# Softmax over the row dot products of two batches: VectorE sums all 32 rows of a step

## The chip, the core and the metric

The kernel runs on one core of a Trainium2 chip. The core has several engines that run their own instruction streams and meet at semaphores: VectorE (DVE in the profile) and ScalarE (ACT) do the arithmetic here, SyncE (SP) orders the transfers between the chip's memory (HBM) and the on-chip memory, and 16 DMA engines carry them out. TensorE is not used. On-chip memory has 128 partitions; a tile of 128 x 512 has 512 elements in each.

The metric is the device time of one execution in microseconds, as a median over runs.

## The reference

```python
B, N, D = 8, 4096, 512          # x and y: B x N x D, float32
gram = np.matmul(x, y.transpose(0, 2, 1))
diag = np.diagonal(gram, axis1=1, axis2=2)
diag = diag - diag.max(axis=-1, keepdims=True)
exp = np.exp(diag)
return (exp / exp.sum(axis=-1, keepdims=True)).astype(np.float32)
```

Only the diagonal of the product is kept, so what is computed is, for each of 8 x 4096 rows, the dot product of a row of x with the same row of y (512 elements), and then a softmax over the 4096 values of each batch. Both inputs, 134 MB together, have to be read once; the output has 0.13 MB.

## The kernel before

Four batches are worked on at a time. A batch's 4096 rows are spread over a quadrant of 32 partitions, 128 rows to a partition (C = 128), so that the four batches fill 128 partitions. Two such groups of batches make the whole. A step t takes R = 32 rows of each partition; there are S = 8 steps, 0 to 3 for the first group and 4 to 7 for the second. A step loads 32 x 512 elements per partition of x (8.4 MB over all partitions) and as much of y.

Buffers: x has two buffers (xs, used in turn: t % 2), y has one (ys). A small buffer, side, holds the last K = 6 rows of y of a step. The tile diag holds the dot products, 128 columns per group; res holds the results.

Steps 0 to 5 are the loop at L133. In each of them

- SyncE orders the load of x (L71) into the buffer of this step, and then the load of y (L74). Both are on one queue, in the order of the program. The order of x waits until the sums of step t - 2, which read the same buffer, are done; the order of y waits until the first multiply of step t - 1 and the copy to side have read ys.
- ScalarE copies the last 6 rows of y to side (L136), as soon as y has landed.
- VectorE multiplies the first 26 rows of x by y, in place (L78, 13,312 elements per partition), and then the last 6 rows by side (L78, 3,072 elements). So ys is free after the first of the two.
- The products are summed along each row. VectorE sums rows 0 to 29 in one instruction (sums, L81, a reduce of 15,360 elements per partition to 30 values). ScalarE sums rows 30 and 31 (sums_act, L86; W = 2), each with one activation that copies the row onto itself and accumulates, and an instruction that reads the accumulator out to diag.

Behind the sums of step 3 VectorE takes the maximum of the first group (L106, L100) and ScalarE the exponentials (L113); step 4 begins on VectorE with the normalization (L100, L119, L120).

Steps 6 and 7 stand outside the loop. In step 6 the rows of y that are kept aside go to the part of the other x buffer that step 7 fills last (spare, L150), and ScalarE sums 30 rows, VectorE two. The first piece of x of step 7 (15 rows) is ordered, as in the loop, when the sums of step 5 are done. Step 7 loads x and y in pieces and takes the dot products row by row on VectorE (L89), so that little is left to do when the last piece lands. Then the second group's softmax and the stores follow.

The instructions of each engine run in the order in which the program writes them; nothing reorders them. An order of a transfer that has to wait holds up what SyncE orders behind it.

Of the kernel before, what the change touches and what calls it, by code (L numbers as in the profile page):

```python
# [11 lines left out]
def kernel(  # L12
# [17 lines left out]
    R = 32  # L30
    H = R // 2
    K = 6
    W = 2
# [30 lines left out]
    def rows(t, r0, n):  # L64
        return xs[t % 2][:, r0 : r0 + n, :]

    def dots_of(t, r0, n):
        return diag[t * R // C][:, columns(t, r0, n)]

    def load_x(t, r0, n):  # L70
        nc.sync.dma_start(out=rows(t, r0, n), in_=xv[t * R // C, :, columns(t, r0, n), :])  # L71

    def load_y(t, r0, n):
        nc.sync.dma_start(out=ys[:, r0 : r0 + n, :], in_=yv[t * R // C, :, columns(t, r0, n), :])  # L74

    def products(t, r0, n, yt):
        xt = rows(t, r0, n)
        nc.vector.tensor_tensor(out=xt, in0=xt, in1=yt, op=Alu.mult)  # L78

    def sums(t, r0, n):  # L80
        nc.vector.tensor_reduce(out=dots_of(t, r0, n), in_=rows(t, r0, n), axis=X, op=Alu.add)  # L81

    def sums_act(t, r0, n):
        for r in range(r0, r0 + n):
            row = xs[t % 2][:, r, :]
            nc.scalar.activation(out=row, in_=row, func=Act.Copy, accum_out=dots_of(t, r, 1))  # L86
# [21 lines left out]
    def exps(i, d):  # L108
        mxp = small.tile([P, 1], f32, name=f"mxp{i}")
        largest(mxp, d)  # L110
        nmx = over_quadrant(f"nmx{i}", mxp, Alu.max, negate=True)
        sump = small.tile([P, 1], f32, name=f"sump{i}")
        nc.scalar.activation(out=res[i], in_=diag[i][:, :C], func=Act.Exp, bias=nmx, scale=1.0, accum_out=sump)  # L113
        return sump

    def normalize(i, sump):
        total = over_quadrant(f"sum{i}", sump, Alu.add)
        rc = small.tile([P, 1], f32, name=f"rc{i}")
        nc.vector.reciprocal(out=rc, in_=total)  # L119
        nc.vector.tensor_single_scalar(out=res[i], in_=res[i], scalar=rc, op=Alu.mult)  # L120
# [12 lines left out]
    for t in range(S - 2):  # L133
        load_x(t, 0, R)
        load_y(t, 0, R)
        nc.scalar.activation(out=side, in_=ys[:, R - K :, :], func=Act.Copy)  # L136
        if t == C // R:
            normalize(0, sump)
        products(t, 0, R - K, ys[:, : R - K, :])
        products(t, R - K, K, side)  # L140
        sums(t, 0, R - W)
        sums_act(t, R - W, W)
        if t == C // R - 1:
            sump = exps(0, diag[0])

    t = S - 2
# [78 lines left out]
```

## Time and profile before

| | |
|---|---|
| Median of 3 runs | 319.71 us |
| Runs, lowest to highest | 319.66 to 319.84 us |
| Span of the profiled execution | 318.4 us |
| HBM read over the span | 134.22 MB, 422 GB/s |

The page gives no other time of the profiled execution than its span, from the first to the last instruction; the runs' times hold what lies ahead of it and behind it as well, 1.3 us more at the median.

The page begins with the busy time of each engine and the span in 40 slices: each digit is the busy share of a slice in tenths, 9 is 90% or more. For the DMA line that is the mean over the 16 DMA engines. "q1" is the queue on which all loads run. The chain of waits follows the work that ended last back from the last instruction: each piece is work, or a wait for a transfer. A transfer's piece in it runs from its order to its landing, and that includes the time in which it stands in the queue behind others.

In the views that group instructions a row has the line, the engine, the operation, output and input tile, shapes and count; then busy time and mean ns of one, and the idle time just before them. In the view in order of time a row starts with start and duration in us; idle time before the instruction stands in brackets at the end with what ended it.

### The profile page before, as it was taken

What the parts mean: (1) busy time and instruction counts of PE and PEld (TensorE: products, weight loads), DVE (VectorE), ACT (ScalarE), POOL (GpSimd) and SP (SyncE); (2) the same over time, 40 slices, a digit from 0 to 9 for tenths busy, and PEclk for the clock granted to TensorE, in tenths of its full rate; (3) what the DMA queues carried; (4) which work ended last, traced back from release to release, by engine and by line L of the source; (5) the groups of instructions that cost most, each with busy time, mean ns of one, the idle gap of its engine ahead of it and who ended that gap; (6) DMA issues with size and microseconds to landing.
All of it is one profiled execution on the core that took longest, in us unless ns stands there. A gap on an engine that the chain in (4) does not pass through costs nothing.

```text
span 318.4 us, 320 instructions
## 1 busy us (share of the span) xinstructions
DVE 241.7 (76%) x101; ACT 49.8 (16%) x97; POOL 0.2 (0%) x4
## 2 busy tenths in 40 slices
DVE  0000079994899939999399994999939998499995
ACT  1000030100301003010020102101030100496700
POOL 0000000000000000000000000000000000000000
DMA  9999999999999999999999999999999999999993
GB/s 397 395 395 510 412 395 453 469 395 395 486 436 395 453 469 395 395 486 436 395 395 519 403 395 461 461 395 395 527 395 395 486 436 395 425 415 432 434 410 140
DMA packets 3970, 134.37 MB, mean 422 GB/s; under 512 B 512, under 2 KB 896, under 8 KB 1536
## 3 DMA queue, kind: packets, MB, share of 16 engines
q1 hardware_dynamic: 3824, 134.29, 97.9%
q10 hardware_dynamic: 144, 0.07, 0.1%
q14 instruction: 2, 0.02, 0.0%
HBM read 134.22 MB, written 0.13 MB: 422 GB/s over the span
## 4 chain that ended last, share of the span: by engine, by line
DMA 70%; DVE 28%; issue 0%; SPq 0%; ACT 0%; DVEq 0%
DMA ys<-in_y_dram 59%; DVE xs L78 28%; DMA xs<-in_x_dram 11%; DVE xs L89 0%; SPq L74 0%; SPq L71 0%; DVE res L120 0%; DVE nmx L100 0%; DVE sum L100 0%; ACT res L113 0%; DVE mxp L106 0%; DVE rc L119 0%; DVEq L78 0%; DVEq L89 0%; SPq L131 0%
## 5 line engine op out<-in xcount | busy, mean ns | idle before, releaser
L78 DVE TENSOR_TENSOR xs<-xs,ys 128x13312 f32<-128x13312 f32 (+2 forms) x8 | 96.7, 12091 | 70.3 <-DMA ys<-in_y_dram 70.3
L81 DVE TENSOR_REDUCE diag<-xs 128x30 f32<-128x15360 f32 (+1 forms) x7 | 98.1, 14020 | 0.2
L86 ACT ACTIVATE xs<-xs 128x512 f32<-128x512 f32 x42 | 25.9, 617 | 90.4 <-DVE xs L78 90.4
L136 ACT ACTIVATE side<-ys 128x3072 f32<-128x3072 f32 x6 | 16.6, 2763 | 124.5 <-DMA ys<-in_y_dram 124.5
L89 DVE SCALAR_TENSOR_TENSOR xs<-xs,ys 128x512 f32<-128x512 f32 (+2 forms) x33 | 20.0, 669 | 0.8 <-DMA ys<-in_y_dram 0.7
L78 DVE TENSOR_TENSOR xs<-xs,side 128x3072 f32<-128x3072 f32 x6 | 20.1, 3350 | 0.0
L86 ACT ACTIVATION_READ_ACCUMULATOR xs<-xs 128x1 f32 x42 | 7.8, 187 | 0.0
L150 ACT ACTIVATE xs<-ys 128x4608 f32<-128x4608 f32 x1 | 4.0, 4043 | 19.9 <-DMA ys<-in_y_dram 19.9
L113 ACT ACTIVATE res<-diag,nmx 128x128 f32<-128x128 f32 x2 | 0.8, 401 | 29.8 <-DVE nmx L100 29.8
L78 DVE TENSOR_TENSOR xs<-xs,xs 128x4608 f32<-128x4608 f32 x1 | 5.0, 4951 | 0.0
L89 DVE DVE_READ_ACCUMULATOR xs<-xs,ys 128x1 f32 x33 | 2.7, 81 | 0.0
L124 ACT ACT_TABLE_LOAD x1 | 1.3, 1283 | 0.7 <-PEq L209 0.7
L100 DVE TRANSPOSE_TENSOR_REDUCE sum<-sump 128x1 f32<-128x32 f32 x2 | 0.4, 212 | 1.2 <-ACT res L113 1.2
L128 DVE MEMSET ys<- 128x1 f32 x1 | 0.1, 59 | 1.4 <-PEq L209 1.4
L120 DVE TENSOR_SCALAR res<-res,rc 128x128 f32<-128x128 f32 x2 | 0.6, 286 | 0.1
L106 DVE TENSOR_REDUCE mxp<-diag 128x1 f32<-128x128 f32 (+1 forms) x2 | 0.5, 228 | 0.1
L100 DVE TRANSPOSE_TENSOR_REDUCE nmx<-mxp 128x1 f32<-128x32 f32 x2 | 0.4, 212 | 0.1
L106 DVE TENSOR_REDUCE diag<-diag 128x1 f32<-128x64 f32 (+1 forms) x2 | 0.4, 202 | 0.0
L119 DVE RECIPROCAL rc<-sum 128x1 f32<-128x1 f32 x2 | 0.3, 164 | 0.1
L113 ACT ACTIVATION_READ_ACCUMULATOR res<-diag,nmx 128x1 f32 x2 | 0.4, 186 | 0.0
L189 ACT ACTIVATE met<-diag 128x96 f32<-128x96 f32 x1 | 0.3, 282 | 0.0
L209 POOL MEMSET const-bfloat16-1.0<- 128x1 bf16 x1 | 0.1, 101 | 0.0
(3 smaller groups left out, 0.3 us busy)
## 6 DMA issues: line engine op xcount, KB each, us to landing
ys<-in_y_dram SPq DMA_DIRECT2D x1, 4352.0 KB, 14.8
xs<-in_x_dram SPq DMA_DIRECT2D x1, 3840.0 KB, 14.1
ys<-in_y_dram SPq DMA_DIRECT2D x1, 2304.0 KB, 12.2
xs<-in_x_dram SPq DMA_DIRECT2D x1, 2048.0 KB, 19.3
xs<-in_x_dram SPq DMA_DIRECT2D x1, 1536.0 KB, 15.5
ys<-in_y_dram SPq DMA_DIRECT2D x1, 768.0 KB, 16.9
ys<-in_y_dram SPq DMA_DIRECT2D x3, 256.0 KB, 18.2
xs<-in_x_dram SPq DMA_DIRECT2D x1, 608.0 KB, 18.0
```

Of the source, the lines that this page charges most:

```text
L78: nc.vector.tensor_tensor(out=xt, in0=xt, in1=yt, op=Alu.mult)
L81: nc.vector.tensor_reduce(out=dots_of(t, r0, n), in_=rows(t, r0, n), axis=X, op=Alu.add)
L86: nc.scalar.activation(out=row, in_=row, func=Act.Copy, accum_out=dots_of(t, r, 1))
L89: nc.vector.scalar_tensor_tensor(out=xt, in0=xt, scalar=1.0, in1=yt, op0=Alu.mult, op1=Alu.mult, accum_out=out)
L100: nc.vector.tensor_reduce(out=got, in_=column.to_broadcast([P, G]), axis=X, op=op, negate=negate, apply_transpose=True)
L106: nc.vector.tensor_reduce(out=out, in_=d, axis=X, op=Alu.max)
L113: nc.scalar.activation(out=res[i], in_=diag[i][:, :C], func=Act.Exp, bias=nmx, scale=1.0, accum_out=sump)
L119: nc.vector.reciprocal(out=rc, in_=total)
L120: nc.vector.tensor_single_scalar(out=res[i], in_=res[i], scalar=rc, op=Alu.mult)
L124: nc.scalar.preload_act_table(Act.Exp)
L136: nc.scalar.activation(out=side, in_=ys[:, R - K :, :], func=Act.Copy)
L150: nc.scalar.activation(out=spare, in_=ys[:, F - L : F, :], func=Act.Copy)
```

## The change

In steps 0 to 5 VectorE's sum covers all 32 rows of the step instead of the first 30, and ScalarE's two row sums are taken out. The loads, the multiplies, the copy to side, steps 6 and 7 and the softmax stay as they are.

```diff
         products(t, 0, R - K, ys[:, : R - K, :])
         products(t, R - K, K, side)
-        sums(t, 0, R - W)
-        sums_act(t, R - W, W)
+        sums(t, 0, R)
         if t == C // R - 1:
             sump = exps(0, diag[0])
```

The reduce of a step has 16,384 elements per partition instead of 15,360 and writes 32 values. In six steps 12 activations and 12 accumulator reads go.

## The prediction

> **What bounds the kernel now.** I read the page first: the busy line, the DMA line, the share of the load queue and the chain of waits.
>
> ```profile
> span 318.4 us, 320 instructions
> DVE 241.7 (76%) x101; ACT 49.8 (16%) x97; POOL 0.2 (0%) x4
> DMA  9999999999999999999999999999999999999993
> q1 hardware_dynamic: 3824, 134.29, 97.9%
> DMA 70%; DVE 28%; issue 0%; SPq 0%; ACT 0%; DVEq 0%
> ```
>
> Two readings compete. The chain gives 28% of the span to VectorE, as if VectorE and the loads took turns. The DMA line says that the 16 engines are never under 90% busy until the last slice, and q1, the queue of all loads, fills 97.9% of their span; the missing 2.1% is 6.7 us. Which reading holds, the view by windows decides. Its columns are length, busy time of DVE, ACT and POOL with counts, clock, DMA share, GB/s. I cut it where the first multiply of each step starts.
>
> ```profile
> 2.00:42.00 40.00, 0.00 (x0) 0.02 (x2) 0.00 (x0) 1.00 1.00 433
> 42.06:80.89 38.83, 33.45 (x4) 4.03 (x6) 0.00 (x0) 1.00 1.00 432
> 80.89:119.51 38.62, 33.44 (x4) 4.10 (x6) 0.00 (x0) 1.00 1.00 434
> 158.47:197.30 38.83, 34.60 (x8) 4.64 (x8) 0.00 (x0) 1.00 1.00 432
> ```
>
> With no compute at all (2 to 42 us) the loads run at 433 GB/s, and in the steps, with VectorE busy 33.4 of 38.8 us, at 432 to 434 with share 1.00. A step loads 2 x 32 x 512 x 4 bytes x 128 partitions = 16.78 MB; at 432 GB/s that is 38.84 us, and the measured step is 38.83 us. So the step is the time of its bytes. The VectorE pieces of the chain are the waits of an early order for the next transfer, made while the queue still has work. What matters of an edit to VectorE is therefore one thing: does the queue ever run empty because a load is ordered later?
>
> **The change part by part.** Step 0 and the start of step 1, in order of time (start, duration, engine, line):
>
> ```profile
> 42.06 14.03 DVE L78 TENSOR_TENSOR xs<-xs,ys 128x13312 f32<-128x13312 f32 x1 [40.65 <-DMA ys<-in_y_dram]
> 56.00 3.35 DVE L78 TENSOR_TENSOR xs<-xs,side 128x3072 f32<-128x3072 f32 x1
> 56.17 0.33 SPq L74 DMA_DIRECT2D ys<-in_y_dram  x1
> 59.39 0.63 ACT L86 ACTIVATE xs<-xs 128x512 f32<-128x512 f32 x1 [14.64 <-DVE xs L78]
> 59.39 16.15 DVE L81 TENSOR_REDUCE diag<-xs 128x30 f32<-128x15360 f32 x1
> 60.53 0.19 ACT L86 ACTIVATION_READ_ACCUMULATOR xs<-xs 128x1 f32 x1
> 75.61 0.33 SPq L71 DMA_DIRECT2D xs<-in_x_dram  x1
> 80.89 14.03 DVE L78 TENSOR_TENSOR xs<-xs,ys 128x13312 f32<-128x13312 f32 x1 [5.35 <-DMA ys<-in_y_dram]
> ```
>
> *Removed:* in each of six steps two ScalarE row sums and their accumulator reads, from 59.39 to 60.72, 1.33 us. They run beside the reduce, which starts at the same 59.39 and ends at 75.54. SyncE's x load (L71) waits for both, and the reduce is 14.8 us later, so nothing on the path is removed. ScalarE's next work, the copy to side at 80.88, waits for y. Worth: 0. What the two row sums ordered for ScalarE by standing in its program (that VectorE had finished with side, and, before the copy to spare in step 6, with the old rows of that x buffer) must now be waited for on VectorE's semaphore; those ends, the multiply from side and the reduce, are over 4 us past by then (below), so I price such waits at 0.
>
> *Added:* 1,024 elements per partition to each reduce. The two shapes of that operation in the grouped view by form:
>
> ```profile
> L81 DVE TENSOR_REDUCE diag<-xs 128x30 f32<-128x15360 f32 x6 | 96.9, 16153 | 0.2
> L81 DVE TENSOR_REDUCE diag<-xs 128x2 f32<-128x1024 f32 x1 | 1.2, 1220 | 0.0
> ```
>
> (16,153 - 1,220) / (15,360 - 1,024) = 1.0416 ns an element; 1,024 of them are 1,067 ns, so the reduce of 32 rows takes 17.22 us. That shape isn't in the trace: bounds are 16.15 us from below (the same row with no growth) and 17.37 us from above (16,153 plus a whole two-row reduce of 1,220). I take 17.22, since both rows lie on that line. Six times 1.067 is 6.4 us more of VectorE.
>
> *Who waits for it.* VectorE itself: it ends its reduce at 76.61 in place of 75.54, and its next multiply waits for y until 80.89 anyway. Of the 5.35 us idle shown there 4.28 are left. Step 3 is tighter, since its maximum and exponentials stand behind the reduce, and the normalization of step 4 too:
>
> ```profile
> 193.65 0.28 DVE L120 TENSOR_SCALAR res<-res,rc 128x128 f32<-128x128 f32 x1
> 197.30 14.03 DVE L78 TENSOR_TENSOR xs<-xs,ys 128x13312 f32<-128x13312 f32 x1 [3.37 <-DMA ys<-in_y_dram]
> ```
>
> 3.37 us idle there becomes 2.30. The cover is never gone. Step 5 hands over to step 6, the first after the loop, whose multiply at 274.61 and whose copy to spare at 274.62 wait for y; the reduce of step 5 ends at 269.50, and will at 270.57. From 274.6 on every start is the same, the tail too.
>
> SyncE: the load of x for two steps on, into the buffer just summed, is ordered when the reduce ends: 76.68 in place of 75.61. This is the term that could count, so I bound it. Behind it on the queue stands only the load of y for the next step but one, which waits for a multiply some 19 us later (94.98 below), so it isn't moved. The chain in order of time (start, length, what) gives the landing of y, which is when the queue would be empty; SyncE's orders of x stand between.
>
> ```profile
> 94.98 24.44 DMA ys<-in_y_dram
> 250.11 24.41 DMA ys<-in_y_dram
> ```
>
> ```profile
> 114.43 0.33 SPq L71 DMA_DIRECT2D xs<-in_x_dram  x1
> 269.53 0.33 SPq L71 DMA_DIRECT2D xs<-in_x_dram  x1
> ```
>
> In step 0 x is ordered 80.79 - 75.61 = 5.2 us ahead; the shortest leads are 94.98 + 24.44 - 114.43 = 4.99 in step 1 and 250.11 + 24.41 - 269.53 = 4.99 in step 5. After the change they are 3.92. How much is needed? Nothing in this trace runs with a shorter lead, so I bound it by the launch, where the queue is empty:
>
> ```profile
> 0.83 0.39 SPq L71 DMA_DIRECT2D xs<-in_x_dram  x1
> ```
>
> ```profile
> 0.00:1.00 1.00, 0.00 (x0) 0.28 (x1) 0.20 (x4) 1.00 0.00 0
> 1.00:2.00 1.00, 0.06 (x1) 1.00 (x1) 0.00 (x0) 1.00 1.59 541
> 2.00:3.00 1.00, 0.00 (x0) 0.00 (x1) 0.00 (x0) 1.00 1.34 524
> ```
>
> The order goes out at 0.83 and first packets start between 1.00 and 2.00 (a share above 1 shows that a packet's whole time is put where it starts): at most 1.17 us from order to packet. The 16 engines start within 1.00 to 3.00, so the first to run dry may do so up to 2.0 us ahead of the landing that the last one sets. Worst case: 3.92 - 2.0 = 1.92 us for an engine that needs at most 1.17. There is room of 0.75 us even with both bounds at their bad end. From below the cost is 0 (an earlier order can't pass a full queue, so no gain); from above it is the whole delay, 1.07 us for each of six x loads (steps 2 to 7), 6.4 us. I take 0, as the need from the launch is far below the lead.
>
> A rule of the Trainium skill speaks a little against this: "DMA: Bandwidth & Descriptors", section "Anatomy of one DMA", gives a fixed part of about 2.0 us for a transfer, by its account mostly completion. If all of it stood ahead of the first packet, the estimate by that page would be 2.0 - 1.92 = 0.08 us missing on the first engine in each of six steps, 0.5 us in all, 320.2. The launch row with its 1.17 at most disagrees with such a use of it.
>
> *Sum:* 0 + 0 + 0. The span stays 318.4; the median of the runs, 319.71, lies 1.3 us above it for what is outside the span, which the change doesn't touch. Predicted: 319.7.
>
> **The rivals.**
>
> *The lead is too short (slower).* Place: the join of y and the x load after it, in each step. It decides once an engine needs its order more than 3.92 us ahead of the landing of y, counted with the spread between engines. All leads shown are at or over 4.99, so the trace can't exclude a need between the two: that is for it. Against it is the launch. Each us missing is an idle us of the queue, six times; half of the delay gives 6 x 0.53 = 3.2 us, 322.9, all of it 6.4 us, 326.1.
>
> *The reduce becomes the path on VectorE (slower).* It decides where the reduce of 32 rows takes over 16.15 + 3.37 = 19.5 us, so that step 4's multiply is late, and over 16.15 + 5.1 = 21.3 in the other steps; then y orders slip as well. For it: 28% of the chain is VectorE's. Against it: the two reduce rows leave no room for a jump of 3.4 us over two rows. At 21.5 us it would be 2 us in step 4 and 0.2 in five others, 3 us, 322.7. The Trainium skill, "VectorE: DVE Perf Modes", "Rules for kernel authors", calls tensor_reduce on the hot path the slowest VectorE operation and advises to restructure; charged in full, the estimate by that rule is 6 x 1.07, 326.1. The step windows show that it isn't on the hot path here.
>
> *ScalarE's accesses slowed something (faster).* If the two row sums held up transfers or the reduce, taking them away gives time back. Over 0.64 us would have to come from 8.0 us of ScalarE work, 8% of the rate while it runs. The window without any compute has 433 GB/s, those with ScalarE's 4.0 to 4.6 us have 432 to 434: no such loss. A shorter ScalarE program could also save an instruction fetch beside the first loads:
>
> ```profile
> q14 instruction: 2, 0.02, 0.0%
> ```
>
> Two packets at the launch, 0.0% of the engines' span: even a whole us saved ends at 318.7, and I expect none.
>
> **How the numbers follow.** No change that can be told: 0.90. Lead too short: 0.05; the reduce on the path or another wait on VectorE: 0.02; faster: 0.03. A measurement of this kernel tells about 0.2%, 0.64 us, from no change, so "same" is 319.07 to 320.35. The range is the likeliest case's own, 319.2 to 320.3: below by the spread of the runs (0.18 us) and a small gain at the launch, above by the estimate of half a us of dry queue. Outside lies under 0.1.
>
> **What would show it.** Right: six reduces of 128x16384 at about 17,220 ns, x orders 1.07 us later (76.7, 115.5, 270.6), VectorE idle ahead of the multiplies 4.0 to 4.3 us (2.3 at 197.3), steps still 38.6 to 39.0 us at 432 GB/s, ScalarE with 24 instructions fewer and about 42 us busy. Wrong: a step longer than 39.0 us with a DMA share below 1.00 around the landing of y (lead), or a multiply that starts after its y landed without an idle gap before it (VectorE on the path), or a first multiply that starts clearly off 42.06 (launch).

## The result and the profile after

| | before | changed |
|---|---|---|
| Median, same chip | 319.84 us (11 runs) | 320.46 us (11 runs) |
| Lowest to highest | 319.60 to 320.23 | 319.82 to 320.73 |
| Ratio of the runs | | 1.0019, 95% interval 1.0011 to 1.0027 |
| Span of the profiled execution | 318.4 us | 319.0 us |

The changed kernel is 0.6 us slower, outside the predicted range by 0.16 us. A second measurement on another occasion (below) gave 1.0012, interval 1.0003 to 1.0021, with 320.26 us. The effect is as small as a measurement of this kernel can tell, but its sign is clear in both.

The page of the changed kernel first, the busy line, the load queue and the chain's shares:

```profile
span 319.0 us, 289 instructions
DVE 248.1 (78%) x101; ACT 41.8 (13%) x73; POOL 0.2 (0%) x4
q1 hardware_dynamic: 3824, 134.29, 97.8%
DMA 70%; DVE 28%; issue 0%; SPq 0%; ACT 0%; DVEq 0%
```

VectorE has its 6.4 us more, ScalarE 8.0 us and 24 instructions less. Chain and queue look as before, though the end is later. In order of time, around the end of step 0 and the start of step 1:

```profile
59.60 17.22 DVE L81 TENSOR_REDUCE diag<-xs 128x32 f32<-128x16384 f32 x1
76.85 0.33 SPq L71 DMA_DIRECT2D xs<-in_x_dram  x1
80.86 2.76 ACT L136 ACTIVATE side<-ys 128x3072 f32<-128x3072 f32 x1 [35.90 <-DMA ys<-in_y_dram]
80.87 14.03 DVE L78 TENSOR_TENSOR xs<-xs,ys 128x13312 f32<-128x13312 f32 x1 [4.05 <-DMA ys<-in_y_dram]
```

The reduce takes the predicted 17.22 us, the x order goes out at 76.85 (before: 75.61), and the multiply starts at 80.87 as it did (80.89). The first multiply of this execution starts at 42.28 in place of 42.06; in two later profiles of the kernel before it starts at 42.21 and 42.29, so that isn't the change. The loss comes later and in small pieces. The chain in order of time shows y's pieces:

```profile
56.39 24.39 DMA ys<-in_y_dram
94.96 24.60 DMA ys<-in_y_dram
172.67 25.15 DMA ys<-in_y_dram
```

The second lands at 94.96 + 24.60 = 119.56, 0.14 us later than before (119.42); the one of 25.15 us lands at 197.82, and the multiply behind it starts at 197.91, where it started at 197.30. By windows, cut at the multiplies, and that multiply's row in order of time:

```profile
80.87:119.66 38.79, 34.52 (x4) 2.77 (x2) 0.00 (x0) 1.00 1.00 433
158.58:197.91 39.33, 35.67 (x8) 3.26 (x4) 0.00 (x0) 1.00 0.99 427
```

```profile
197.91 14.03 DVE L78 TENSOR_TENSOR xs<-xs,ys 128x13312 f32<-128x13312 f32 x1 [2.92 <-DMA ys<-in_y_dram]
```

39.33 us is over the 39.0 that I had named as the sign of a queue running dry, with a share of 0.99; VectorE is idle for 2.92 us ahead of the multiply, so it isn't VectorE. But the sign doesn't tell the two kernels apart: in two later profiles of the changed kernel no step is longer than 38.95 us, and one profile of the kernel before has a step of 39.01. The single packets tell more.

The trace also holds a record of every DMA packet, with start, duration and size. In steps 0 to 6 a load is eight packets of 64 KB on each of the 16 engines, and a packet takes 2.42 us as a rule. I counted those that took over 2.6 us (from 6 us to 285 us of the span), and where they lie, in this profile and in those taken in the experiments below:

```
                                     packets over 2.6 us   of them behind a just ordered x load
before, three profiles                      0, 0, 0
changed, three profiles                     7, 11, 14             6, 11, 14
```

In the changed kernel the long packets are the first ones of an x load (2.61 to 3.27 us), starting 2.6 to 3.7 us after its order. In the kernel before the first packets of x are like all others. One packet of the first profile, at 186.92 us and 3.36 us long, lies in the midst of a y load; it makes most of the 39.33 us there, none like it is in the other two profiles, and why it was long stays open.

### The profile page after: what moved, and what is told of

Same layout as the page of the kernel before. It is cut to its first block, busy times and chain, and to the rows that moved or that the text cites. A ratio compares the mean times of both kernels' runs of the same rounds, so it can differ in the third digit from the quotient of the medians.

```text
span 319.0 us, 289 instructions
## 1 busy us (share of the span) xinstructions
DVE 248.1 (78%) x101; ACT 41.8 (13%) x73; POOL 0.2 (0%) x4
## 4 chain that ended last, share of the span: by engine, by line
DMA 70%; DVE 28%; issue 0%; SPq 0%; ACT 0%; DVEq 0%
DMA ys<-in_y_dram 59%; DVE xs L78 28%; DMA xs<-in_x_dram 11%; DVE xs L89 0%; SPq L74 0%; SPq L71 0%; DVE res L120 0%; DVE sum L100 0%; DVE nmx L100 0%; ACT res L113 0%; DVE mxp L106 0%; DVE rc L119 0%; DVEq L78 0%; DVEq L89 0%; SPq L131 0%
## 5 line engine op out<-in xcount | busy, mean ns | idle before, releaser
L81 DVE TENSOR_REDUCE diag<-xs 128x32 f32<-128x16384 f32 (+1 forms) x7 | 104.5, 14934 | 0.2
L86 ACT ACTIVATE xs<-xs 128x512 f32<-128x512 f32 x30 | 18.4, 614 | 2.8 <-DVE xs L78 2.8
L86 ACT ACTIVATION_READ_ACCUMULATOR xs<-xs 128x1 f32 x30 | 5.6, 187 | 0.0
```

## The experiments

Theory A: the x order, 1.07 us later, comes too late for some DMA engines, which run out of packets or start the next load slowly. Theory B: it is ScalarE's absence, by waits or by its shorter program. Theory C: something else that goes with the longer reduce. A "join" is the place on the queue where a load of y ends and the load of x behind it begins. "Lead" is the time from the x order to the start of the next multiply, which comes 0.1 us after y has landed; each lead below is the range over the six x loads of one profile.

**The kernel before once more.**

> The kernel before once more, as a control with its spans. Every theory: 319.7 to 319.9 us, ratio 1.000 within 0.05%. What it settles: if the time less the span is 1.3 us here and 1.75 us in the changed kernel (320.73 with a span of 319.0), then part of the 0.6 us lies outside the span; if it is about 1.75 us here too, all of it lies inside, and the spans differ by 0.6.

319.79 us, ratio 1.0001 (0.9992 to 1.0010), span 318.4 with a time of 320.21 in the profiled execution. Over its 11 executions the span runs from 317.7 to 318.6, and the time lies 1.7 to 1.8 us above the span in each; in the changed kernel also 1.7 to 1.8. So the whole loss lies in the span, and the profile shown before was of an execution some 0.4 us slower than the typical one: my 1.3 us had mixed a median with one execution's span.

**ScalarE off or on, reduce short or long.** Two kernels fill the square; both edits are shown against the changed kernel.

```diff
+    for d in diag:
+        nc.vector.memset(d, 0.0)
...
-        sums(t, 0, R)
+        sums(t, 0, R - W)
```

> ScalarE's two row sums are left out and VectorE still sums 30 rows, so rows 30 and 31 of steps 0 to 5 are not summed (their dot products are set to zero once at the start). The x order goes out after the reduce of 16.15 us, as in the kernel before, about 5 us ahead of the landing of y. Theory A (the later x order costs the 0.6 us): 319.8, ratio 1.000. Theory B (ScalarE's absence costs it, by waits or by the layout of its program): 320.4, ratio 1.002.

319.75 us, ratio 1.0002 (0.9993 to 1.0011), with no packet over 2.6 us in its profile.

```diff
+    spill = small.tile([P, W], f32, name="spill")
...
         sums(t, 0, R)
+        for i in range(W):
+            nc.scalar.activation(
+                out=side[:, i, :], in_=xs[t % 2][:, R - W + i, :], func=Act.Copy, accum_out=spill[:, i : i + 1]
+            )
```

> VectorE sums 32 rows as in the changed kernel, and ScalarE still does two row sums a step, now into a scratch row and two scratch values that nobody uses. The x order goes out after the reduce of 17.22 us. Theory A (late x order): 320.4, ratio 1.002. Theory B (ScalarE's absence): 319.8, ratio 1.000.

320.21 us, ratio 1.0014 (1.0004 to 1.0024), with 12 long packets, all at the joins. With ScalarE gone and the reduce short nothing is lost; with ScalarE kept and the reduce long it is lost. The two intervals still overlap a little; the long packets in the two profiles, none against 12, say the same more clearly. Theory B falls.

**The x load in halves.** To keep the long reduce and give the order its lead back, x is loaded (steps 0 to 6) and summed (steps 0 to 5) in halves; a control does the same to the kernel before.

```diff
-        load_x(t, 0, R)
+        load_x(t, 0, R // 2)
+        load_x(t, R // 2, R // 2)
...
-        sums(t, 0, R)
+        sums(t, 0, R // 2)
+        sums(t, R // 2, R // 2)
```

> VectorE sums all 32 rows, ScalarE none, as in the changed kernel, but in two reduces of 16 rows, and x is loaded in two halves of 16 rows, each ordered when its half is summed. The first half is ordered some 8.5 us earlier than in the changed kernel and the second half at about the same time as there, with 4.2 MB (9.7 us) more ahead of it. Theory A (late x order): 319.8, ratio 1.000. Theory B (ScalarE's absence): 320.4. If packets of 32 KB cost something by themselves, more than that.

320.28 us, ratio 1.0014 (1.0006 to 1.0023): a miss by theory A's number. The control decides what it means.

> The kernel before (ScalarE sums two rows), with x loaded in halves and VectorE's sum split into rows 0 to 15 and 16 to 29, as in the experiment on halves. It measures what the halves cost by themselves where the lead was ample already. If the halves cost nothing: 319.8, and then the 320.28 of the changed kernel with halves speaks against theory A. If the halves cost the 0.45 us by themselves: 320.3, and then with halves the changed kernel has lost nothing to the reduce, as theory A has it.

320.37 us, ratio 1.0013 (1.0004 to 1.0022). The halves cost about 0.5 us by themselves, in the kernel before as well, and in halves the changed kernel is no slower than the kernel before. In order of time, the changed kernel in halves:

```profile
59.35 17.27 DVE L81 TENSOR_REDUCE diag<-xs 128x16 f32<-128x8192 f32 x2
68.05 8.92 SPq L71 DMA_DIRECT2D xs<-in_x_dram  x2
80.91 14.03 DVE L78 TENSOR_TENSOR xs<-xs,ys 128x13312 f32<-128x13312 f32 x1 [4.29 <-DMA ys<-in_y_dram]
```

The first half is ordered at 68.05, 12.9 us ahead; the reduces together last as long as the one of the changed kernel. Neither of the two kernels has a slow packet at a join: the 32 KB packets of x take 1.21 us as a rule and 1.32 us at most. So a reduce of that length costs nothing where the order isn't late, which is against theory C.

**More and less lead.** VectorE sums n rows once more behind the reduce, or ScalarE takes more or fewer rows.

```diff
+    again = small.tile([P, n], f32, name="again")
...
         sums(t, 0, R)
+        nc.vector.tensor_reduce(out=again, in_=rows(t, 0, n), axis=X, op=Alu.add)
```

> The changed kernel, and behind the reduce of 32 rows VectorE sums the first two rows once more into values that nobody uses (1.22 us). So the x order goes out 1.2 us later than in the changed kernel, 2.4 to 2.7 us ahead of the landing of y; VectorE still has over 1.5 us idle ahead of each multiply. Theory A (an x order that comes late leaves DMA engines without work): the need lies just above the lead of the changed kernel, so another 1.2 us are missing; a gap in one step gives the next step its lead back, so it counts in about three of six: 320.5 + 3.6, some 324 (321.5 to 325). Theory C (the 0.6 us come from something else that goes with the longer reduce or the altered program, and the lead is ample): 320.4 to 320.6.

> The same with four rows summed once more (2.29 us): the x order goes out 1.3 to 1.6 us ahead of the landing of y; VectorE still has 0.6 us idle or more ahead of each multiply. Theory A: 320.5 + 3 x 2.3, some 327 (324 to 329). Theory C: 320.4 to 320.6.

> The changed kernel with one row summed once more (0.7 us), a point between the changed kernel (320.46, x ordered 3.6 to 4.1 us ahead of the landing of y) and two rows again (325.44, some 2.7 us). Lead about 3.2 us. Theory A with a need that spreads over some 1.5 to 4.5 us from engine to engine: 322 to 324. If instead the loss jumps at one threshold: near 320.6 or near 325.4.

```diff
-        sums(t, 0, R - W)
-        sums_act(t, R - W, W)
+        sums(t, 0, R - n)
+        sums_act(t, R - n, n)
```

> The kernel before with four rows a step summed by ScalarE in place of two, and 28 by VectorE: the x order goes out about 7 us ahead of the landing of y in place of 5. Theory A, if the need is at or below 5 us: 319.8, ratio 1.000; if even a lead of 5 us costs something now and then: 319.6, and fewer runs above 320. Theory B and C: 319.8.

> The kernel before with one row a step on ScalarE and 31 on VectorE: the x order goes out about 4.5 us ahead of the landing of y, between the kernel before (5.0 to 5.2) and the changed one (3.6 to 4.1). Theory A: between 319.8 and 320.4; nearer to 319.8 if the longest need that occurs is about 4.4 us.

| kernel | lead, us | median, us | ratio, 95% interval | packets over 2.6 us |
|---|---|---|---|---|
| ScalarE 4 rows | 6.1 to 6.2 | 320.06 | 1.0007 (0.9998 to 1.0016) | 0 |
| before (control) | 5.1 to 5.5 | 319.79 | 1.0001 (0.9992 to 1.0010) | 0 |
| ScalarE 1 row | 4.5 to 4.6 | 319.73 | 1.0003 (0.9994 to 1.0012) | 2 |
| changed | 4.0 to 4.8 | 320.46 | 1.0019 (1.0011 to 1.0027) | 7 |
| one row again | 3.4 to 4.5 | 322.88 | 1.0114 (1.0086 to 1.0142) | 24 |
| two rows again | 2.9 to 5.6 | 325.44 | 1.0172 (1.0158 to 1.0186) | 67 |
| four rows again | 1.8 to 3.5 | 326.46 | 1.0206 (1.0182 to 1.0230) | 52 |

The last three rows have four runs each, up to 2.7 us apart; the others have 11. The curve is flat down to 4.5 us and bends at about 4: 1.2 us more on VectorE moved the changed kernel by 5.0 us, where the change itself had moved it by 0.6. Theory C, which gave 320.5 for both of the repeated sums, falls. It isn't VectorE's path either: even with four rows again VectorE waits 1.75 us or more for y ahead of every multiply. That a lead over 5 us isn't worth anything is shown too (6.1 us: no gain). What two rows again look like: the join in order of time and the same stretch by windows, once in the control and once here.

```profile
76.80 1.21 DVE L144 TENSOR_REDUCE again<-xs 128x2 f32<-128x1024 f32 x1
78.03 0.33 SPq L73 DMA_DIRECT2D xs<-in_x_dram  x1
80.94 14.02 DVE L80 TENSOR_TENSOR xs<-xs,ys 128x13312 f32<-128x13312 f32 x1 [2.94 <-DMA ys<-in_y_dram]
```

The control:

```profile
56.00:78.00 22.00, 19.66 (x3) 1.34 (x4) 0.00 (x0) 1.00 1.00 435
78.00:90.00 12.00, 9.07 (x1) 2.76 (x1) 0.00 (x0) 1.00 1.01 437
```

Two rows again:

```profile
56.00:78.00 22.00, 21.96 (x4) 0.00 (x0) 0.00 (x0) 1.00 1.01 438
78.00:90.00 12.00, 9.06 (x2) 2.76 (x1) 0.00 (x0) 1.00 0.91 366
```

From 78 to 90 us the DMA share falls from 1.01 to 0.91 and the rate from 437 to 366 GB/s, while VectorE does the same work. By the packet records seven of the 16 engines run out of packets at this join and stand idle for 9.6 us taken together, and the first packets that follow are slow as well (up to 3.6 us). VectorE's idle gap of 2.94 us ahead of the multiply shows that it isn't VectorE. The chain in order of time then has y's pieces by turns long and short:

```profile
56.45 24.41 DMA ys<-in_y_dram
95.03 26.82 DMA ys<-in_y_dram
136.03 24.44 DMA ys<-in_y_dram
174.65 27.08 DMA ys<-in_y_dram
215.91 24.89 DMA ys<-in_y_dram
```

That is the feedback that its expectation named: what the queue loses at one join delays the next y (95.03 + 26.82), and so gives the next x order its lead back (2.9, 5.3, 2.9, 5.6 us). It loses 2.4 and 2.7 us at the first and the third join, more than the 1.2 that the order was later. An engine that started late ends late: the engines, which in the control end a load within 0.7 us of each other, here need up to 3.3 us (packet records). That is the likely reason why the 324 expected here (321.5 to 325) was too low; four rows again (327 expected) and one row again (322 to 324) came as expected.

**Why does an order need so long?** One idea: it has to get past packets of 64 KB in hand. Each y load is ordered in four (steps 0 to 6), 16 KB a packet, first in the kernel before and then with the late order.

```diff
-        load_y(t, 0, R)
+        for q in range(4):
+            load_y(t, q * R // 4, R // 4)
```

> The kernel before with each load of y in steps 0 to 6 ordered as four loads of 8 rows at the same place, so packets of 16 KB in place of 64 KB. It measures what the quarters cost by themselves, where the x order has 5 us of lead: 319.9 to 321.

> Two rows summed once more, as in the run with 325.44, with y in quarters as in the kernel above. What is open is why an order needs over 1.2 us. Theory A1 (the order has to get past what the engines have in hand, so its first packet waits for packets of 64 KB that take 2.42 us each): with packets of 16 KB ahead of it, the first packet comes sooner and most of the 5.6 us goes: within 2.5 us of the time of the quarters alone. Theory A2 (the time from order to first packet under load is what it is, whatever the packets): 5 to 6 us above the time of the quarters alone.

321.12 us, ratio 1.0040 (1.0024 to 1.0056), for the quarters alone, a little more than expected, and 327.18 us, ratio 1.0228 (1.0205 to 1.0250), with the late order: 6.1 us apart, where 64 KB packets had 5.7 (325.44 against 319.76 in the same batch). Theory A1 falls: with packets of a quarter the loss is no smaller. What else makes an order slow was not settled. One more thing stands in the packet records of two rows again. At the first join, where seven engines had run dry and nine had not, the seven got their first packet of x 2.69 to 4.42 us after the order. At the fifth, where 14 had run dry, these got it after 0.96 to 1.48 us, nearly as at the launch. That points to a need that depends on what the other engines are doing; two joins don't prove it, and the reason stays open.

**Where the changed kernel's own loss lies.** The longest packet of its first profile wasn't at a join (theory D: such packets make the loss, and have nothing to do with the order). Two more profiles of it and one of the kernel before decide.

> The changed kernel once more, for a second profile and a second interval. Theory A: ratio 1.001 to 1.003, and packets of over 2.6 us among the 64 KB packets of steps 0 to 6 are the first ones of an x load, starting 2 to 4.5 us after its order. Theory D (an occasional long packet in the midst of a transfer, which has nothing to do with the order, makes the loss): they lie anywhere.

> As above, a third profile of the changed kernel. Theory A: long packets at the first packets of x loads alone. Theory D: anywhere in the transfers.

> The kernel before, a third profile. Theory A: no packet over 2.6 us in steps 0 to 6. Theory D: one or two, anywhere.

320.26 us, ratio 1.0012 (1.0003 to 1.0021); the third profile of each is of a single execution, 320.03 us and, for the kernel before, 319.71. All 11 and 14 long packets of the changed kernel are first packets of an x load, starting 2.7 to 3.7 us after its order, and the kernel before has none. The lone packet at 186.92 did not come again. Theory A holds for the changed kernel; a share of theory D in its first profiled execution remains. The size fits too, as far as it can be told: what the first packets of x take over 2.42 us adds up to 0.3 us an execution when spread over the 16 engines, in each of the three profiles, and to 0.1 or less in the kernel before. That this is the whole 0.4 to 0.6 us isn't shown, since a landing waits for the last engine alone. Packets of 2.43 to 2.6 us in the midst of loads come in both kernels: in the two profiles of the kernel before with a span of 318.4 they add up to 0.6 us an engine, in the one with 317.9 to almost nothing, in the three of the changed kernel to 0.4, 0.1 and 0.1.

## Why the prediction was wrong

The bound of the kernel was read rightly: time is the loads' time, VectorE's pieces of the chain are waits made while the queue has work. ScalarE's part is worth 0, as said (319.75 us with it taken out alone). The reduce of 32 rows takes 17,220 ns, as worked out from two rows. VectorE has 4.04 to 4.38 us idle ahead of its multiplies (4.0 to 4.3 predicted). In step 4 it has 2.92, where 2.30 was predicted and y came 0.6 us later; in the two later profiles it has 2.18 and 2.27. The x orders went out 1.0 to 1.6 us later than before, by 1.07 and by what had been lost until then.

The step that failed is the bound on how much lead an order needs: "at most 1.17 us from order to packet", and from it "room of 0.75 us even with both bounds at their bad end". Two things were wrong in it. First, I took the launch's earliest packet for the need of every engine. The same rows show packets starting between 2.00 and 3.00 us as well; by the packet records of that launch the 16 engines begin 1.0 to 2.1 us after the order. An engine that is first to run dry can be last to be served, and with 2.1 in place of 1.17 the bad end is 1.92 - 2.1, no room at all. Secondly, the launch is an empty machine. In the kernel with two rows again, where engines ran dry and their next packets show when service came, those packets start 0.96 to 4.42 us after the order, and the latest are at a join where nine of the 16 engines were at work throughout. The curve bends between leads of 4.5 and 4.0 us; in the changed kernel the first engine ends its y at 79.68, 1.2 us ahead of the multiply (less than the 2.0 us that I had allowed for the spread), so that is 2.8 to 3.3 us ahead of the first engine's end, well inside 0.96 to 4.42. The leads that I had, 4.99 before and 3.92 after, lay on both sides of the bend; I had written that the trace can't exclude a need between the two, and gave that 0.05.

The rival named the mechanism, and over-priced it. Half the delay at each of six joins was to give 3.2 us; measured are 0.4 to 0.6. At this lead at most six engines of 16 at a join are served late, mostly by a slow first packet (0.2 to 0.9 us over) rather than by a gap, and engines that were ahead can lose that without moving the landing, which the last one sets. A loss of 3 us and more came only with orders another 0.6 to 1.2 us later (322.88, 325.44).

The estimate that I made by the Trainium skill, "DMA: Bandwidth & Descriptors", "Anatomy of one DMA" (fixed part of 2.0 us, 320.2 us), came within 0.3 us of the result, and I set it aside on the strength of the launch row. That section gives the figure for transfers that GpSimd orders, which I left out; the loads here are ordered by SyncE. It was near by chance: the measured times from order to first packet spread on both sides of 2.0 us.

## What to carry to other kernels

Where the queue of loads is the bound, the number to guard is the lead of each order over the moment at which the queue would be empty, and the shortest lead without loss in the trace is a bound that is known; a need derived from an idle launch isn't. Here an order 0.5 us later cost nothing, one 1.1 us later 0.4 to 0.6 us in all, and one 2.3 us later 5.7 us, so price a late order by a curve, made with a repeated piece of work behind which the order waits. And work that lies in an engine's idle time isn't free as long as something else waits for its end.

## What the runs showed of the hardware

- From an order to the first packet on an engine: 1.0 to 2.1 us at the launch of the kernel before (up to 2.4 in other profiles); with two rows again 0.96 to 1.48 us where 14 of 16 engines had run dry and 2.69 to 4.42 us where seven had. The Trainium skill, "DMA: Bandwidth & Descriptors", "Latency and other measured facts", gives about 600 ns to the first byte for transfers ordered as here (HWDGE). Counted from the start of the order no run here shows as little (0.87 us at the least, for the store that ScalarE orders at the end); from the end of that ordering instruction it is 0.5 us.
- First packets of a load whose order came late take up to 3.3 us in the changed kernel, where a 64 KB packet takes 2.42 us as a rule.
- Loads in smaller pieces cost by themselves here: x in halves (32 KB a packet) 0.13% (0.04 to 0.22), y in quarters (16 KB) 0.40% (0.24 to 0.56), with the queue full.
